# Chunked linear attention of the first half moved into the second input projection, with a first chunk's load one step ahead of its scores

## The chip, the core and the metric

The kernel runs on one NeuronCore of a Trainium2 chip: TensorE (PE, with its weight loads shown as PEld), VectorE (DVE), ScalarE (ACT), GpSimd (POOL), and SyncE (SP), whose queue issues the DMAs here. The metric is the device time of one execution in microseconds (us); lower is better. Times are compared as medians of several runs on one chip, and a profile shows one execution.

## The reference

One decoder block over 2048 positions of width 1024, all in float32. A normalised input goes through one input projection; its columns feed a gated linear attention (four heads, a forget gate of low rank) and a short gated convolution; both are joined by an output projection, and a gated feed-forward network follows.

```python
proj = h @ w_in[l]
p_q, p_k, p_v, p_g, p_a, c_b, c_c, c_h = jnp.split(proj, splits, axis=-1)
gate_logits = p_a @ w_gate_up[l] + b_gate[l]
log_a = jax.nn.log_sigmoid(gate_logits) / GATE_NORMALIZER
o = gla_chunked(q, k, v, log_a)
o = rmsnorm(o, gla_norm_g[l]) * jax.nn.silu(p_g)
u = c_c * c_h
o_conv = c_b * causal_depthwise_conv(u, conv_w[l])
x = x + jnp.concatenate([o_gla, o_conv], axis=-1) @ w_out[l]
h2 = rmsnorm(x, norm2_g[l])
x = x + (jax.nn.silu(h2 @ w_ffn_gate[l]) * (h2 @ w_ffn_up[l])) @ w_ffn_down[l]
return rmsnorm(x, norm_f_g)
```

Within a chunk the scores q k^T are masked and multiplied with v, and a state carried from chunk to chunk adds `q_t S_t`. The kernel uses chunks of 128 positions.

## The kernel before

The sequence is worked on in two halves of 1024 positions, each of two blocks of 512 (`b` = 0, 1 and 2, 3). Every product of a large matrix is a Strassen-like product of seven smaller ones (`PRODUCTS`: A11·B11, S1·T1, S2·T2, A12·B21, S3·T3, S4·B22, A22·T4), and each float32 factor is split into a high and a low part (`split`: ScalarE writes the high part, VectorE the rest), so that one product step is three matmuls (lines 447 to 449).

`unit` does the seven products for two column tiles of the weights: it loads 1 MB of raw weights (`raw`), mixes and splits them into seven quarters (`wq`), and multiplies each with one of the seven sorts of operand (`op`, four tiles each, 28 in all, in a pool `opp` of 28 slots). A product of the input projection is 12 matmuls, a unit 84. `in_proj(half)` runs over the units: k, q, two of v, two of g, then twice cc, ch, cb of the convolution. The first half has its first two units in a special opening, so `in_proj(0)` runs ten and `in_proj(1)` twelve. In the first half VectorE mixes the weights, in the second GpSimd.

The operands of the second half (`h1_ahead`) are made beside the first half's projection and kept in DRAM (`siB`, `siT`); `load_pairs(s_h1)` loads them back between the two projections. Since `opp` is full, each such load waits until the last unit of `in_proj(0)` has used the slot. The sorts T3, B22 and T4 are kept whole (256 KB) and split again after loading (`load_whole`); the others come as pairs (512 KB).

The attention of a half is a generator, `gla_half`. A chunk has three steps with a `yield` behind each: `gla_scores` (`sc` matmuls, masked copies into `scores` on VectorE, transposes `kt_ps` and `v_ps`, on ScalarE their evictions and the scaled state `carry`), `gla_outputs` (`o_ps`, `kv`, the new state, the norm), and `gla_finish` (transpose `ot`, gate, split, two stores to `sgla`). `gla_load` issues 14 DMAs of 64 KB for a chunk (`kq`, `ee`, `vt`, `gt`), and computes the exponentials of the decay and their products with k and q. `gate(half)` makes the decays of a half: 32 matmuls `a_ps`, four `z`, and for each `z` a chain of ScalarE and VectorE work with a scan (`forget_gate`), stored to `sd`.

What runs beside the projections stands in the list `background`, one generator after the other. Each product of a unit calls `tick`, which counts `pace` and, at every second product, does one step of the first generator in the list; `steady` adds a step at every fourth. A scheduler then sets the order of all instructions on each engine, by the program's order and its own model of time; engines keep that order. All DMAs here go through SyncE's one queue, in order.

Before the change, `gla_half(0)` is put into the list within `in_proj(0)`, after the g units, behind `h1_paced()`; its first three steps fall into the last unit of that projection. `gate(1)` comes next, at the start of `in_proj(1)`, and `gla_half(1)` follows after the g units of `in_proj(1)`; it ends within the output projection of the first half (`out_proj(0)`, four quarters of 96 matmuls). `out_proj(1)` reads what it stored.

Of the kernel before, what the change touches and what calls it, by code (L numbers as in the profile page):

```python
# [53 lines left out]
def tile_hymba_block(ctx, tc, x, xt, win, wa, wgu, wout, wffn, wdown, wdown_first, small, out):  # L54
# [83 lines left out]
    def bank(name="mm"):  # L138
        return ps.tile([P, PB], F32, name=name, tag="mm")
# [10 lines left out]
    def store(dst, src):  # L150
        return nc.sync.dma_start(dst, src)
# [5 lines left out]
    @contextmanager  # L157
    def behind(marks):

        with ExitStack() as stack:  # L160
            for m in marks:
                stack.enter_context(tc.issue_after(m.ins))
            yield
# [94 lines left out]


    background = []  # L260
    pace, ahead, hurry, steady = [0], [], [], []

    def step():
        while background:
            try:
                next(background[0])
                return
            except StopIteration:
                background.pop(0)

    def tick():
        pace[0] += 1
        if ordered:
            return
        if pace[0] % 2 == 0 or hurry:
            step()
            if steady and pace[0] % 4 == 0:
                step()
        elif ahead and pace[0] % 4 == 1:
            next(ahead[0], None)  # L280

# [9 lines left out]
    def unhurried():  # L291
        hurry.clear()
        steady.append(True)
        yield

    def h1_paced():
        with_marks.append(True)
        yield from h1_ahead()
        with_marks.clear()
        steady.clear()  # L300

    def drain_background(until=lambda: False):
        while background and not until():
            step()
# [210 lines left out]
    def settled(c, in_psum):  # L515

        if not in_psum:
            return c
        s = tt("c11")
        act.activation(s[:], c[:], AF.Copy)  # L520
        return s
# [3 lines left out]
    def silu(c, in_psum):  # L525
        s = tt("sg") if in_psum else c
        last_silu[:] = [act.activation(s[:], c[:], AF.Silu)]
        return s
# [404 lines left out]
    def gate(half, ops, mark=None):  # L933

        a = bank("a_ps")
        names = "B11", "T1", "B21", "B22"
        with behind([mark] if mark else []):
            for n in names:  # L940
                for k in range(4):
                    q = {"B11": 3 * k + 1, "T1": 3 * k, "B21": 2 * k + 13, "B22": 2 * k + 12}[n]
                    w = wa_sb[:, 32 * q : 32 * q + P]
                    for e in range(2):
                        pe.matmul(  # L945
                            a[:], w, ops[n][k][:, e, :],
                            start=(n, k, e) == ("B11", 0, 0),
                            stop=n == "B22" and k == 3 and e == 1, skip_group_check=True,
                        )
        if mark:  # L950
            yield

        stacks = []
        if half == 0:
            second_factor()
        for j in range(2):
            stack = bx[0].tile([96, PB], F32R, name="a_sb", tag="b")
            r, low = [slice(32 * n, 32 * n + 32) for n in (j, 1 - j)]
            with behind(held):
                act.activation(stack[r, :], a[r, :], AF.Copy)  # L960
                act.activation(stack[64:96, :], a[r, :], AF.Copy)
                dve.tensor_tensor(stack[low, :], a[r, :], stack[r, :].bitcast(F32), ALU.subtract)
            stacks.append(stack)
        yield
        for j in range(2):
            small = decays[2 * half + j] = [
                mtiny.tile([P, 2, PT], F32, name=n, tag=n, bufs=4) for n in ("em", "dn", "el")
            ]
            for i in range(2):
                z = bank("z")  # L970
                pe.matmul(
                    z[:], wgu_sb[:, i * P : (i + 1) * P], stacks[j][:], start=True, stop=True
                )
                forget_gate(2 * half + j, i, z, *small)
                yield
# [20 lines left out]
    def in_proj(half, ops, raw=None, between=(), rest=None):  # L996
        def units():
            if half == 0:
                yield unit(win[2], ops, raw=raw, between=between, rest=rest)
            for u in range(0 if half else 3, 12):  # L1000
                yield unit(win[u], ops, eng=pool if half else dve)

        units = units()
        for dst, i0 in ((s_kq, 0), (s_kq, 2), (s_v, 0), (s_v, 2)):
            if half == 0 and dst is s_kq:
                continue
            for r, j, c, p in next(units):
                store(dst[2 * half + j][i0 + r][:], settled(c, p)[:])
        for i0 in (0, 2):
            for r, j, c, p in next(units):  # L1010
                store(s_g[2 * half + j][i0 + r][:], silu(c, p)[:])
        background.append(gla_half(half))
        for i0 in (0, 2):
            cc = {(r, j): settled(c, p) for r, j, c, p in next(units)}
            ch = {(r, j): c for r, j, c, _ in next(units)}
            for r in range(2):
                i = i0 + r
                left = halo[:, i, :]
                for j in range(2):
                    s = tp.tile([P, PB + 2], F32, name="u", tag="t")  # L1020
                    dve.tensor_tensor(s[:, 2:], ch[r, j][:], cc[r, j][:], ALU.mult)
                    act.activation(s[:, 0:2], left, AF.Copy)
                    left = s[:, PB : PB + 2]
                    y = cc[r, j]
                    act.activation(y[:], s[:, 0:PB], AF.Copy, scale=col(C_CW + i))
                    for n in (1, 2):
                        dve.scalar_tensor_tensor(
                            y[:], s[:, n : n + PB], col(C_CW + 4 * n + i), y[:], ALU.mult, ALU.add
                        )
                if half == 0:  # L1030
                    act.activation(halo[:, i, :], left, AF.Copy)
            for r, j, c, _ in next(units):
                y = cc[r, j]
                dve.tensor_tensor(y[:], c[:], y[:], ALU.mult)
                hi = tp.tile([P, PB], F32R, name="hi", tag="t")
                split(y[:], hi[:], y[:].bitcast(F32R))
                dst = s_mix[2 * half + j][i0 + r]
                store(dst[:, 0, :], hi[:].bitcast(F32))
                store(dst[:, 1, :], y[:])


    def gla_half(half):
        chunks = [(b, t) for b in (2 * half, 2 * half + 1) for t in range(PT)]
        with tc.issue_after(last_silu[0].ins):
            tables = act.preload_act_table_set("natural_log_exp_and_others")
        with tc.issue_after(tables.ins):
            nxt = gla_load(*chunks[0])
        o = None
        for n, (b, t) in enumerate(chunks):
            cur = nxt  # L1050
            s = gla_scores(b, t, *cur)
            yield
            if o is not None:
                gla_finish(*chunks[n - 1], *o)
                yield
            if n + 1 < len(chunks):
                nxt = gla_load(*chunks[n + 1])
            o = gla_outputs(b, t, *s)
            yield
        gla_finish(b, t, *o)  # L1060
        done.add((b, t))
        yield
# [4 lines left out]
    def gla_load(b, t):  # L1067
        s = slice(t * P, (t + 1) * P)
        kq, e, vt, g = [bt(n, (P, 4, P)) for n in ("kq", "ee", "vt", "gt")]
        for dst, src in ((kq, s_kq[b]), (e[:, 2:4, :], s_d[b]), (vt, s_v[b]), (g, s_g[b])):  # L1070
            for i, r in enumerate(src):
                load(dst[:, i, :], r[:, s])
        act.activation(e[:, 0:2, :], e[:, 2:4, :], AF.Exp, scale=-1.0 / 16.0)
        act.activation(e[:, 2:4, :], e[:, 2:4, :], AF.Exp, scale=1.0 / 16.0)
        dve.tensor_tensor(kq[:, 0:2, :], kq[:, 0:2, :], e[:, 0:2, :], ALU.mult)
        dve.scalar_tensor_tensor(
            kq[:, 2:4, :], kq[:, 2:4, :], 0.125, e[:, 2:4, :], ALU.mult, ALU.mult
        )
        return kq, e, vt, g
# [412 lines left out]
    ops, raw, between, steps, rest = opening()  # L1492
# [4 lines left out]
        ]  # L1497
    )
    in_proj(0, ops, raw, between, rest)
    drain_background(lambda: len(background) < 2)  # L1500
    ops = load_pairs(s_h1)
    background.append(gate(1, ops))
    in_proj(1, ops)
    drain_background(lambda: (1, PT - 1) in done)
    ssq = out_proj(0, build_mix(0))
# [118 lines left out]
```

## Time and profile before

| what | us |
|---|---|
| median of 3 runs | 2073.3 |
| lowest and highest run | 2071.59, 2073.36 |
| the profiled execution | 2071.13 |
| its span (first to last instruction) | 2069.4 |
| TensorE busy in it | 2029.7 |
| VectorE, ScalarE, GpSimd busy | 1426.7, 971.2, 774.1 |

The mean granted TensorE clock of that execution is 0.994 of full speed. A row of a timeline reads: start and length in us, engine, source line, operation, tile written <- tiles read, shapes, count; in square brackets the idle time of the engine before it and what ended that. In a table of windows each row gives, for a stretch of time, busy us and number of instructions of PE, PEld, DVE, ACT and POOL, then the granted clock, the mean busy share of the 16 DMA engines and the GB/s they moved. "SPq" is SyncE's queue issuing a DMA. Line numbers are those of the kernel before.

### The profile page before, as it was taken

The numbers are of one execution on the slowest core, as the hardware profiler recorded it, in microseconds if no ns is written. First come the engines' busy times: TensorE is split into PE (matmuls) and PEld (weight loads), VectorE is DVE, ScalarE is ACT, GpSimd is POOL, SyncE is SP. The second block draws the span as 40 slices with busy tenths as digits, with TensorE's granted clock in tenths as the row PEclk, the third lists the DMA queues.
The fourth block names the chain that finished last, engine by engine and source line by source line (L and its number), as shares of the span: only waits on it lengthen the run. The fifth ranks groups of instructions, "written<-read, shape, count | busy, mean of one in ns | idle before, by whom it ended". The sixth has DMA issues, their size and how long they took to land.

```text
span 2069.4 us, 27151 instructions
## 1 busy us (share of the span) xinstructions
PE 2029.7 (98%) x9271; PEld 1666.8 (81%) x9271; DVE 1426.7 (69%) x2185; ACT 971.2 (47%) x1930; POOL 774.1 (37%) x566
## 2 busy tenths in 40 slices
PE   9999989999999999999999999999999999999997
PEld 8778768887888888888888888787888888878786
DVE  7878966568753686776676577776766666667774
ACT  6765555665542344444444452334434444453344
POOL 0000012222102474564564345533644554434544
PEclk9999999999999999999999999999999999999998
DMA  7356695434587783555454576477454444486653
GB/s 259 123 188 213 231 336 183 142 107 148 169 311 282 258 285 123 186 193 180 169 190 163 194 285 245 180 282 283 143 188 163 154 162 168 171 308 223 239 215 126
DMA packets 189739, 422.54 MB, mean 204 GB/s; under 512 B 19904, under 2 KB 65184, under 8 KB 180128
## 3 DMA queue, kind: packets, MB, share of 16 engines
q1 hardware_dynamic: 189600, 420.81, 57.3%
q8 instruction: 73, 1.20, 0.2%
q14 instruction: 66, 0.54, 0.1%
HBM read 276.02 MB, written 144.70 MB: 203 GB/s over the span
## 4 chain that ended last, share of the span: by engine, by line
PE 86%; DVE 6%; DMA 3%; ACT 2%; issue 1%; SPq 0%; POOL 0%; DVEq 0%; ACTq 0%
PE mm L447 24%; PE mm L449 24%; PE mm L448 24%; PE mm L1186 3%; PE mm L1189 3%; PE mm L1187 3%; DVE wq L194 1%; DMA op<-shT 1%; DMA op<-sa_B 1%; DVE op L194 1%; PE mm L731 1%; PE a_ps L945 1%; PE mm L733 1%; PE mm L732 1%; PE o_ps L1110 1%
## 5 line engine op out<-in xcount | busy, mean ns | idle before, releaser
L447 PE MATMUL mm<-op,wq 128*128 128x512 f32 x2467 | 963.6, 393 | 17.8 <-ACT wq L193 5.9
L448 PE MATMUL mm<-op,wq 128*128 128x512 f32 x2467 | 962.3, 390 | 2.4 <-DVE op L194 2.4
L449 PE MATMUL mm<-op,wq 128*128 128x512 f32 x2467 | 950.4, 390 | 0.9 <-DVE wq L194 0.8
L194 DVE TENSOR_TENSOR wq<-raw,wq 128x512 fp32r<-128x512 f32 (+2 forms) x612 | 489.3, 804 | 269.2 <-ACT wq L193 265.9
L193 ACT ACTIVATE wq<-raw 128x512 fp32r<-128x512 f32 (+2 forms) x612 | 355.9, 587 | 593.1 <-PE mm L449 453.9
L447 PEld LDWEIGHTS mm<-op,wq 128*128 128x128 f32 x2467 | 463.9, 188 | 123.1 <-ACT wq L193 8.6
L448 PEld LDWEIGHTS mm<-op,wq 128*128 128x128 f32 x2467 | 464.2, 188 | 101.4 <-DVE op L194 6.9
L449 PEld LDWEIGHTS mm<-op,wq 128*128 128x128 f32 x2467 | 464.1, 188 | 99.5 <-DVE wq L194 2.3
L422 POOL TENSOR_TENSOR s<-raw 128x512 f32<-128x512 f32 (+2 forms) x87 | 114.7, 1319 | 455.9 <-DVE wq L194 311.0
L422 POOL TENSOR_TENSOR raw<-raw 128x512 f32<-128x512 f32 (+2 forms) x174 | 228.7, 1320 | 122.8 <-DVE wq L194 117.5
L422 POOL TENSOR_TENSOR raw<-s,raw 128x512 f32<-128x512 f32 (+2 forms) x87 | 112.0, 1288 | 434.2 <-DVE wq L194 397.8
L476 DVE TENSOR_TENSOR c<-mm,c 128x512 f32<-128x512 f32 x196 | 134.4, 686 | 78.2 <-PE mm L449 76.6
L476 DVE TENSOR_TENSOR y<-mm,y 128x512 f32<-128x512 f32 x185 | 126.8, 687 | 83.9 <-PE mm L449 83.3
L1168 POOL TENSOR_TENSOR ssx<-ssx,q 128x512 f32<-128x512 f32 x52 | 76.9, 1493 | 155.4 <-ACT q L1167 155.1
L487 ACT ACTIVATE c<-mm 128x512 f32<-128x512 f32 x198 | 116.1, 588 | 17.2 <-PE mm L449 14.1
L1186 PE MATMUL mm<-op,wq 128*128 128x512 f32 x256 | 100.5, 394 | 0.0
L1187 PE MATMUL mm<-op,wq 128*128 128x512 f32 x256 | 99.7, 389 | 0.0
L193 ACT ACTIVATE wq<-s 128x512 fp32r<-128x512 f32 (+2 forms) x96 | 56.2, 585 | 86.1 <-PE mm L449 85.0
L194 DVE TENSOR_TENSOR wq<-s,wq 128x512 fp32r<-128x512 f32 (+2 forms) x96 | 81.3, 847 | 3.0 <-ACT wq L193 2.3
L194 DVE TENSOR_TENSOR op<-op 128x512 fp32r<-128x512 f32 x94 | 75.1, 828 | 8.3 <-ACT op L193 8.3
L1189 PE MATMUL mm<-op,wq 128*128 128x512 f32 x256 | 79.7, 390 | 0.0
L1381 POOL TENSOR_TENSOR y<-x,y 128x512 f32<-128x512 f32 x32 | 53.8, 1680 | 45.9 <-DVE y L476 41.7
(231 smaller groups left out, 1848.3 us busy)
## 6 DMA issues: line engine op xcount, KB each, us to landing
raw<-in_wffn_dram SPq DMA_DIRECT2D x44, 1024.0 KB, 5.9
sa_B<-so SPq DMA_DIRECT2D x47, 512.0 KB, 4.3
op<-sa_B SPq DMA_DIRECT2D x47, 512.0 KB, 7.0
raw<-in_win_dram SPq DMA_DIRECT2D x22, 1024.0 KB, 5.3
sa_T<-so SPq DMA_DIRECT2D x44, 512.0 KB, 4.4
op<-sa_T SPq DMA_DIRECT2D x44, 512.0 KB, 6.8
raw<-in_wdown_dram SPq DMA_DIRECT2D x24, 768.0 KB, 5.4
sx<-y SPq DMA_DIRECT2D x48, 256.0 KB, 3.8
```

The lines of the kernel that those rows point to most:

```text
L193: last_hi[:] = [act.activation(hi, src, AF.Copy)]
L194: last_lo[:] = [dve.tensor_tensor(lo, src, hi.bitcast(F32), ALU.subtract)]
L422: eng.tensor_tensor(*args)
L447: pe.matmul(o[:], wh, xh, start=first and k == 0, stop=False, skip_group_check=True)
L448: pe.matmul(o[:], wh, xl, start=False, stop=False, skip_group_check=True)
L449: return pe.matmul(o[:], wl, xh, start=False, stop=k == n - 1, skip_group_check=True)
L476: last_plus[:] = [dve.tensor_tensor(t[:], o[:], t[:], ALU.add)]
L487: last_out[:] = [act.activation(t[:], o[:], AF.Copy)]
L1168: pool.tensor_tensor(ssq[:], ssq[:], q[:], ALU.add)
L1186: pe.matmul(o[e, j][:], wh, m[:, 0, :], start=k == 0, stop=False)
L1187: pe.matmul(o[e, j][:], wh, m[:, 1, :], start=False, stop=False)
L1189: pe.matmul(o[e, j][:], wl, ops[k][j][:, 0, :], start=False, stop=k == KD - 1)
```

## The change

`gla_half(0)` is no longer put into the list within `in_proj(0)`. It is put there at the start of `in_proj(1)`, behind three empty steps (`pause(3)`) and ahead of `gate(1)`. While its first 14 steps run, a flag `hasty` adds a step at every fourth product, so three of four products carry one; after that it goes on at every second. And `gla_half`, of either half, gives up its turn once after the first chunk's load, so that the load and the scores of a first chunk are two steps.

```diff
-    pace, ahead, hurry, steady = [0], [], [], []
+    pace, ahead, hurry, steady, hasty = [0], [], [], [], []
@@ tick
             if steady and pace[0] % 4 == 0:
                 step()
+        elif hasty and pace[0] % 4 == 3:
+            step()
         elif ahead and pace[0] % 4 == 1:
             next(ahead[0], None)
@@
+    def pause(n):
+        for _ in range(n):
+            yield
+
+    def hastened(steps, n):
+        hasty.append(True)
+        for i, _ in enumerate(steps):
+            if i == n:
+                hasty.clear()
+            yield
@@ in_proj
-        background.append(gla_half(half))
+        if half:
+            background.append(gla_half(half))
@@ gla_half
             nxt = gla_load(*chunks[0])
+        yield
         o = None
@@
-    drain_background(lambda: len(background) < 2)
+    drain_background()
     ops = load_pairs(s_h1)
-    background.append(gate(1, ops))
+    background.extend([pause(3), hastened(gla_half(0), 14), gate(1, ops)])
     in_proj(1, ops)
```

The scheduler moves more than these lines say. Three places show it.

SyncE's queue, near the end of `in_proj(0)`, as a piece of the difference. `kq` and `ee` are loads of the first chunk, `siB` and `siT` the DRAM copies of the second half's operands.

```order
 L148 DMA kq<-sk_0_113 128x128
 L148 DMA kq<-sk_1_114 128x128
+L148 DMA op<-siB_0_441 128x1024
+L148 DMA op<-siB_1_442 128x1024
+L148 DMA op<-siB_2_443 128x1024
 L148 DMA kq<-sk_2_115 128x128
+L151 DMA siB_3_456<-lo 128x512
+L151 DMA siT_3_468<-t_2506 128x512
+L148 DMA op<-siB_3_444 128x1024
+L148 DMA op<-siT_0_445 128x1024
+L148 DMA op<-siT_1_446 128x1024
```

The operand loads, which stood behind all loads of the first two chunks, now stand behind two of the first chunk's.

SyncE's queue a little later, around the raw weights of the second unit of `in_proj(1)`. Before:

```order
L148 DMA gt<-sg_1_154 128x128
L148 DMA gt<-sg_2_155 128x128
L148 DMA gt<-sg_3_156 128x128
L148 DMA raw<-in_win_dram 128x2048
L148 DMA kq<-sk_0_113 128x128
```

and now, as a piece of the difference:

```order
+L148 DMA op<-siB_0_461 128x512
+L148 DMA op<-siB_1_462 128x512
+L148 DMA op<-siB_2_463 128x512
+L148 DMA raw<-in_win_dram 128x2048
+L148 DMA op<-siB_3_464 128x512
```

Before, these weights stood behind all operands and behind the fourteen loads of the third chunk; now they stand ahead of the last B22 operand (`siB_3_464`) and of the four T4 operands.

TensorE, at the product of the first unit of `in_proj(1)` that reads the T4 operands. The numbers tell the tiles apart: `wq_3059` and `wq_3062` are the last two quarters of that unit before the change, and `wq_2939` is the last one now; `wq_3053` is the second quarter of the unit after it. Before:

```order
L447 MATMUL mm_3080<-op_3017,wq_3059 128x512
L448 MATMUL mm_3080<-op_3017,wq_3059 128x512
L449 MATMUL mm_3080<-op_3017,wq_3059 128x512
L447 MATMUL mm_3065<-op_3021,wq_3062 128x512
L448 MATMUL mm_3065<-op_3021,wq_3062 128x512
L449 MATMUL mm_3065<-op_3021,wq_3062 128x512
```

and now (lines 460 to 462 are the same three as 447 to 449):

```order
L461 MATMUL mm_3110<-op_2848,wq_3053 128x512
L462 MATMUL mm_3110<-op_2848,wq_3053 128x512
L1107 MATMUL kt_ps_3131<-ident_87,kq_3086 128x128
L1110 MATMUL v_ps_3134<-ident_87,vt_3088 128x128 x4
L460 MATMUL mm_2942<-op_2898,wq_2939 128x512
L461 MATMUL mm_2942<-op_2898,wq_2939 128x512
```

The product with T4 followed the product with B22 directly; now the first two products of the next unit and the first chunk's scores and transposes stand between. From the first chunk's scores in the order before (in the last unit of `in_proj(0)`, behind that unit's first product), 143 matmuls of the projections lie before the last B22 operand is read in the new order, 156 before the first chunk's scores, and 168 before the first T4 operand. TensorE's order is the same in both up to those first scores, and from the feed-forward network on the order is the same again.

## The prediction

> **What bounds the kernel now.** I read the engine totals first, then what TensorE waited for between 240 and 480 us (the stretch in which the moved steps run), then that stretch cut into windows, then the instructions there.
>
> ```profile
> span 2069.4 us, 27151 instructions
> PE 2029.7 (98%) x9271; PEld 1666.8 (81%) x9271; DVE 1426.7 (69%) x2185; ACT 971.2 (47%) x1930; POOL 774.1 (37%) x566
> ```
>
> TensorE sets the time and is idle for only 2069.4 - 2029.7 = 39.7 us. A change that moves work and removes none can win only idle time, and time at a reduced clock. What TensorE waited for in the stretch (engine, line, releaser: us in total, times, longest):
>
> ```profile
> PE sc L1086 <- DVE kq L1076: 4.4, 2, 2.5
> PE mm L447 <- ACT wq L193: 4.0, 1, 4.0
> PE mm L448 <- DVE op L194: 1.8, 4, 0.8
> PE mm L447 <- ACT op L193: 1.2, 1, 1.2
> PE mm L447 <- DVE c L476: 0.6, 1, 0.6
> ```
>
> Two waits of the scores (one at the first chunk of each half), one for a weight split, several for the splitting of the next operands, and a short one for an eviction. The long ones lie here:
>
> ```profile
> 250.36 0.71 PE L1086 MATMUL sc<-kq 64*128 64x128 f32 x8 [1.89 <-DVE kq L1076]
> 295.48 0.50 PE L447 MATMUL mm<-op,wq 128*128 128x512 f32 x1 [1.21 <-ACT op L193]
> 307.01 0.50 PE L447 MATMUL mm<-op,wq 128*128 128x512 f32 x1 [4.04 <-ACT wq L193]
> 317.47 0.71 PE L1086 MATMUL sc<-kq 64*128 64x128 f32 x8
> 467.87 1.21 PE L1086 MATMUL sc<-kq 64*128 64x128 f32 x8 [2.47 <-DVE kq L1076]
> ```
>
> The windows (busy us and instructions of PE, PEld, DVE, ACT, POOL; then the granted TensorE clock, DMA share, GB/s):
>
> ```profile
> 240.00:248.00 8.00, 8.00 (x36) 6.42 (x35) 8.00 (x11) 3.74 (x9) 3.30 (x2) 1.00 0.67 233
> 248.00:260.00 12.00, 10.11 (x62) 8.04 (x61) 10.78 (x21) 7.73 (x21) 0.00 (x0) 1.00 0.52 141
> 260.00:296.00 36.00, 33.27 (x160) 25.29 (x158) 25.91 (x48) 20.75 (x48) 3.40 (x2) 1.00 1.03 392
> 296.00:304.00 8.00, 6.55 (x29) 4.38 (x29) 4.54 (x9) 4.31 (x8) 0.00 (x0) 0.79 0.65 182
> 304.00:312.00 8.00, 4.99 (x25) 4.51 (x26) 5.01 (x5) 3.14 (x10) 4.47 (x3) 0.79 0.92 272
> 451.00:466.00 15.00, 14.40 (x64) 11.54 (x62) 14.91 (x27) 11.43 (x27) 6.21 (x4) 1.00 0.46 157
> 466.00:472.00 6.00, 4.13 (x20) 3.49 (x21) 4.72 (x12) 3.68 (x9) 0.00 (x0) 0.72 0.47 134
> ```
>
> Three things are to be seen. From 260 to 296 us the DMA engines are full (share 1.03 at 392 GB/s), while before it they are half idle (0.52). After the stalls the clock is cut (0.79, 0.79, 0.72). And VectorE is full in 240 to 248 and 451 to 466 us (14.91 of 15). Why DMA starts late, and why the weights come late, stands in SyncE's queue:
>
> ```profile
> 257.17 1.86 SPq L148 DMA_DIRECT2D gt<-sg  x4
> 259.13 1.81 SPq L148 DMA_DIRECT2D op<-siB  x4
> 292.17 1.02 SPq L148 DMA_DIRECT2D op<-siT  x2
> 293.56 2.24 SPq L148 DMA_DIRECT2D kq<-sk  x4
> 299.36 1.85 SPq L148 DMA_DIRECT2D gt<-sg  x4
> 301.25 0.43 SPq L148 DMA_DIRECT2D raw<-in_win_dram  x1
> ```
>
> The next half's operands are first asked for at 259.13, behind the small loads of two chunks; the weights on which TensorE waits until 307.01 at 301.25, behind the fourteen loads of a third.
>
> **How much is lost there now.** In 240 to 248 us 36 large matmuls fill 8.00 us, 0.222 us each. From the end of work before the first scores (250.36 - 1.89 = 248.47) to the scores of the fourth chunk at 317.47 TensorE does this much of them:
>
> ```profile
> 248.47:317.47 69.00, 47.29 (x181) 0.95 0.89 308
> ```
>
> (of tile mm alone) 181 x 0.222 = 40.2 us. What the steps of a chunk take, by the pieces of the chain of waits around 500 to 520 us:
>
> ```profile
> 501.70 0.22 PE o_ps L1112 x2
> 501.93 0.59 PE kv L1117 x8
> 508.18 0.65 PE sc L1086 x8
> 508.82 0.37 PE kt_ps L1092 x2
> 509.19 0.44 PE v_ps L1095 x4
> 515.12 0.44 PE ot L1146 x4
> ```
>
> With eight of the o_ps pieces a chunk is 8 x 0.22 + 0.59 + 0.65 + 0.37 + 0.44 + 0.44 = 4.3 us; the first chunk has half the o_ps work, 3.4. Between those two points lie chunks 0, 1 and the third without its ot: 3.4 + 4.3 + 3.8 = 11.5 us. So 69.0 - 40.2 - 11.5 = 17.3 us are lost in one half-to-half boundary.
>
> **The change, part by part.** No matmul is added or dropped; the chunks' 11.5 us are done later, at the same price, so moving them is worth nothing by itself. (1) First scores of the first half: they move 156 matmuls on, their load is far ahead, and the 1.89 us wait goes. It is part of the 17.3.
>
> (2) The boundary. Operand loads now stand ahead of all but two of the first chunk's small loads. Each waits until the last unit of the first projection has used its slot; the first is free when that unit's first product ends, about 248.5, so loading starts some 11 us before the 259.13 of now. How soon is it through? The sizes:
>
> ```profile
> op<-siB SPq DMA_DIRECT2D x8, 512.0 KB, 8.3
> op<-siT SPq DMA_DIRECT2D x8, 512.0 KB, 10.0
> op<-siT SPq DMA_DIRECT2D x8, 256.0 KB, 5.9
> op<-siB SPq DMA_DIRECT2D x4, 256.0 KB, 5.1
> raw<-in_win_dram SPq DMA_DIRECT2D x22, 1024.0 KB, 5.3
> ```
>
> The 28 operands are 16 x 512 + 12 x 256 = 11264 KB. Up to the last B22 operand, itself counted, stand 24 of them (10240 KB), the next unit's weights (1024), eleven chunk loads of 64 KB and four 256 KB stores: 12992 KB or 13.3 MB, 34 us at 392 GB/s. From 247.5 that is 281.5, and with ScalarE's and VectorE's split (about 0.6 us each) near 283. TensorE, never waiting, would ask for it 143 matmuls after 248.47, at 280.2. So some 3 us are lost there. The last T4 operand comes 2.5 MB (6.5 us) later, near 289; the new order has put the next unit's first two products ahead of the product that reads T4, which is 168 matmuls on plus 1.5 us of the first chunk: 287.3, or 290 with the 3 us. Bounds: 0 lost, if TensorE itself is held up by 3 us elsewhere; 9, if the small loads among the big ones hold DMA to the mean of 260 to 304 us ((36 x 392 + 8 x 182) / 44 = 354 GB/s, 38 us), with a clock cut behind it. I take 4, nearest to the 3.0 us (1.8 + 1.2) of operand waits that the full DMA engines leave now.
>
> Behind operand loads that wait for TensorE, SyncE now holds the rest of the first chunk's loads, and ScalarE's exponential of that chunk waits for them with the third weight split of the coming unit behind it. About 4.9 MB stand ahead: 12.5 us, so 260; the split is used 105 matmuls on, at 272. It fits.
>
> (3) The weights of the next unit stand ahead of the last B22 operand and not behind T4 and fourteen chunk loads, so they land near 281, some 8 us before their use: the 4.04 us wait and the clock cut behind it (304 to 312 us) go. Both are in the 17.3; together (1) to (3) leave 4 of it: 13.3 us gained.
>
> On the clock: it was not cut in 248 to 260 us after one idle 1.89 us, and it was cut in 296 to 304 us after waits of which none was over 1.21. The Trainium skill (TensorE: Matmul & The Clock Gate, What's actually happening) has the cut come after an idle window of about 3.4 us; the row speaks against that, since broken waits were enough. By the page, waits broken like those expected here would carry no cut, and 4 us would be nearer to 3.
>
> (4) First scores of the second half: their load is now a step ahead, and the last matmul of the forget gates, whose work filled VectorE in 451 to 466 us, stands 84 matmuls (19 us) before them. The 2.47 us wait goes, and the cut (6.0 x (1 - 0.72) = 1.7): 4.2 us.
>
> (5) What it costs. The gates do not vanish: they move into the units whose convolution needs VectorE too. In 451 to 466 they needed all of it and TensorE still lost only 15.00 - 14.40 = 0.6; with the convolution beside them I take 1.5 (0 to 4). The built order has 17 activation-table loads for 15, the two new ones around the exponentials of a chunk between two silu evictions. A load in the trace:
>
> ```profile
> 396.95 0.62 ACT L193 ACTIVATE wq<-raw 128x512 fp32r<-128x512 f32 x1
> 397.59 1.28 ACT L527 ACT_TABLE_LOAD   x1
> 398.88 0.63 ACT L527 ACTIVATE c<-c 128x512 f32<-128x512 f32 x1
> ```
>
> 1.28 us each, 2.6 on ScalarE, in a place where seven such loads now leave TensorE the one wait of 0.6 on c; I take 1 (0 to 2.6). The Trainium skill (ScalarE: Activation LUTs, What ACT_TABLE_LOAD costs) adds a drain and gives about 2.66 us a switch, 5.3 for two; here the next activation starts at 398.88, 1.29 after the load, and the one before it ended at 397.57, so no drain is seen, and the sum goes by 1.28. Last, the hastened steps: o_ps follows its scores after 24 matmuls (5.3 us) where it mostly had 48. I take 1.5 (0 to 5; the rival below says more). The last chunk ends one quarter of the output projection later, with a quarter (96 matmuls, 21 us) left before the next projection; that one reads 1 MB in twelve matmuls (2.7 us), as fast as 392 GB/s brings it, so it needs only a lead, and has one: nothing.
>
> Sum: -13.3 - 4.2 + 1.5 + 1.0 + 1.5 = -13.5 us on an execution of 2071.1 (span 2069.4). That one lay 2.2 under the median of the three runs, 2073.3; so the median should come to 2073.3 - 13.5, about **2060 us**.
>
> **The rivals.** *Full recovery:* nothing is left at the boundary and the costs in (5) are covered: -17.3 - 4.2 + 1 = -20.5, 2053 us. For it: the next unit's products stand ready to fill. Against it: DMA must carry 13 MB in the 32 us that TensorE gives it, at the rate at which it is already full.
>
> *The stall only moves:* the chunks' 11.5 us of TensorE work used to cover loading; without it TensorE reaches the new operands sooner and waits at the full DMA engines for as long as it saved. Then (1) to (3) give nothing, (4) pays for (5), and the time is 2073. For it: share 1.03 already. Against it: the 11 us of earlier start and the half-idle DMA of 248 to 260 us.
>
> *Slower:* at three steps in four, the chain from scores over VectorE's two masked copies and ScalarE's evictions and carries to o_ps no longer fits between them, and TensorE, which keeps its order, waits in every hastened chunk. It decides when that chain takes over 5.7 us (24 matmuls and the ot between). Six chunks at 2.5 us (the longest wait of scores now) and a clock cut of 1.7 each are 25 us, less the 13.5: 2085. For it: scores and o_ps stood this close in few chunks before. Against it: the list of waits above has no row for o_ps, and VectorE is busy for 25.91 of 36 us and ScalarE for 20.75 there.
>
> **How the numbers follow.** A measurement of this kernel tells 0.2% (4 us) from no change. Chances: forecast 0.55 (its own range 2055 to 2066), full recovery 0.12, the stall moves 0.20, slower 0.13. Faster is the first two and a quarter of the third: 0.72; same 0.15; slower 0.13. The range reaches from full recovery into the moved stall and leaves out the slower case and a few in a hundred below: 2053 to 2073.
>
> **What would show it.** Right: no wait of sc on kq in either half; first operand load near 248; DMA full at once behind it; waits on op of 2 to 6 us near 275 to 290; no 4 us wait on wq; 250 to 315 us shorter by about 13 us when the moved chunks are counted. Wrong: operand waits over 10 us, rows of TensorE waiting for scores, carry or vt before o_ps, or VectorE full for 20 us where gates and convolution meet.

## The result and the profile after

| | median, us | lowest to highest | runs |
|---|---|---|---|
| before | 2072.45 | 2069.94 to 2073.36 | 4 |
| changed | 2061.74 | 2059.16 to 2063.03 | 4 |

The ratio is 0.9949, with a 95% interval of 0.9931 to 0.9966: 10.7 us faster, where 2060 was predicted and 13.5 us forecast. The profiled execution took 2061.84 us. Its first lines:

```profile
span 2060.1 us, 27151 instructions
PE 2023.8 (98%) x9271; PEld 1663.5 (81%) x9271; DVE 1429.7 (69%) x2185; ACT 971.3 (47%) x1932; POOL 770.3 (37%) x566
```

The same 9271 matmuls are in a span 9.3 us shorter. TensorE's idle time fell only from 39.7 to 36.3 us; its busy time fell by 5.9, since a matmul at half clock, or one that starts after a wait, counts as longer (0.50 us for the one at 277.42 us below, 0.39 for the next). What TensorE waited for between 230 and 520 us (engine, line, releaser: us in total, times, longest), and in a stretch of the feed-forward network, where the kernel before has no wait at all (770 to 800 us of its trace):

```profile
PE mm L460 <- DVE c L489: 3.4, 4, 1.6
PE mm L460 <- ACT c L500: 2.8, 2, 2.1
PE mm L461 <- DVE op L194: 0.2, 1, 0.2
```

```profile
PE mm L460 <- ACT c L500: 1.8, 1, 1.8
```

The waits of scores, the 4.0 us on weights and nearly all of those on operands are gone. What is left are waits for evictions, on lines 489 (VectorE) and 500 (ScalarE). Windows of the prediction again (busy us and instructions of PE, PEld, DVE, ACT, POOL; then clock, DMA share, GB/s):

```profile
248.00:260.00 12.00, 12.00 (x55) 9.95 (x54) 11.24 (x18) 6.41 (x13) 1.60 (x1) 1.00 0.98 371
260.00:296.00 36.00, 33.63 (x161) 26.30 (x160) 27.16 (x42) 20.51 (x41) 7.44 (x5) 1.00 0.93 328
296.00:304.00 8.00, 8.00 (x44) 6.39 (x43) 5.51 (x11) 5.48 (x19) 2.58 (x2) 1.00 0.95 315
304.00:312.00 8.00, 8.00 (x52) 6.65 (x50) 4.14 (x6) 3.17 (x10) 3.83 (x3) 1.00 0.53 163
466.00:472.00 6.00, 4.44 (x20) 3.33 (x19) 6.00 (x12) 3.25 (x9) 0.00 (x0) 1.00 0.44 137
```

From 248 to 260 us DMA is now almost full (0.98, before 0.52), and 296 to 312 us is full on TensorE at full clock. SyncE's queue shows why:

```profile
243.09 1.68 SPq L148 DMA_DIRECT2D op<-siB  x3
...
271.24 2.57 SPq L148 DMA_DIRECT2D op<-siB  x3
274.06 0.33 SPq L148 DMA_DIRECT2D raw<-in_win_dram  x1
274.79 0.32 SPq L148 DMA_DIRECT2D op<-siB  x1
...
283.45 0.39 SPq L148 DMA_DIRECT2D op<-siT  x1
```

The first operands are asked for at 243.09 (before: 259.13), the next unit's weights at 274.06 (before: 301.25).

**Where the time is lost, by stretch.** For the comparisons below I add up, from the trace, how far the starts of successive matmuls lie apart beyond the distance of an undisturbed one (0.227 us for 512 columns: 250 of them take 56.67 us; 0.110 for the narrow ones of a chunk). This takes in waits and half clock alike. The stretches are in us of each kernel's own span.

| lost, us | to 240 | 240-318 | 318-440 | 440-540 | 540-690 | 690-820 | rest | all |
|---|---|---|---|---|---|---|---|---|
| before | 11.3 | 15.8 | 1.9 | 4.2 | 0.3 | 1.0 | 19.6 | 54.2 |
| changed | 10.9 | 4.2 | 1.0 | 4.6 | 1.0 | 2.9 | 20.4 | 44.9 |

The difference, 9.3, is that of the spans. 11.6 us are won at the boundary of the two projections; about 1.9 are given back at 775 us, and every other stretch is within a microsecond.

### The profile page after: what moved, and what is told of

It reads as the page before. It is cut to its first block, busy times and chain, and to the rows that moved or that the text cites. A ratio compares the mean times of both kernels' runs of the same rounds, so it can differ in the third digit from the quotient of the medians.

```text
span 2060.1 us, 27151 instructions
## 1 busy us (share of the span) xinstructions
PE 2023.8 (98%) x9271; PEld 1663.5 (81%) x9271; DVE 1429.7 (69%) x2185; ACT 971.3 (47%) x1932; POOL 770.3 (37%) x566
## 4 chain that ended last, share of the span: by engine, by line
PE 82%; DVE 8%; DMA 5%; ACT 2%; issue 2%; POOL 1%; SPq 0%; DVEq 0%; ACTq 0%; POOLq 0%
PE mm L460 24%; PE mm L462 23%; PE mm L461 23%; PE mm L1201 2%; PE mm L1202 2%; PE mm L1204 2%; DVE wq L194 1%; DVE op L194 1%; DMA raw<-in_win_dram 1%; DMA op<-shT 1%; DMA op<-siT 1%; DVE h L882 1%; PE a_ps L958 1%; PE mm L744 1%; PE mm L746 1%
```

## The experiments

Three groups: one part of the change alone, the change without one part, and other orders. The ratio is that to the kernel before on the same chip, with its 95% interval; the losses are of one profiled execution each, by the measure above.

| kernel | median | ratio | 240-318 | 318-440 | 440-540 | 540-690 | 690-820 |
|---|---|---|---|---|---|---|---|
| yield_only | 2070.48 | 0.9996 (0.9987 to 1.0004) | 17.8 | 2.0 | 1.5 | 0.0 | 1.1 |
| pool_queue | 2072.88 | 1.0007 (0.9996 to 1.0018) | 19.1 | 1.1 | 2.6 | 0.5 | 1.0 |
| move_plain | 2076.39 | 1.0029 (1.0019 to 1.0039) | 13.4 | 0.7 | 11.6 | 0.1 | 5.1 |
| no_yield | 2063.35 | 0.9962 (0.9950 to 0.9975) | 3.1 | 0.2 | 11.2 | 0.9 | 0.8 |
| no_pause | 2064.49 | 0.9965 (0.9953 to 0.9977) | 12.0 | 1.7 | 1.3 | 0.9 | 0.2 |
| no_haste | 2073.59 | 1.0007 (0.9998 to 1.0015) | 2.2 | 1.2 | 3.4 | 17.1 | 0.5 |
| late_weights | 2068.94 | 0.9988 (0.9978 to 0.9999) | 11.3 | 0.9 | 4.7 | 1.0 | 3.1 |
| after_again | 2060.30 | 0.9958 (0.9945 to 0.9972) | 3.4 | 1.2 | 4.6 | 0.9 | 3.1 |
| gate_first | 2060.86 | 0.9952 (0.9937 to 0.9968) | 1.4 | 5.9 | 0.5 | 0.9 | 4.0 |
| haste_all | 2060.96 | 0.9947 (0.9935 to 0.9959) | 3.5 | 1.9 | 5.7 | 0.9 | 0.4 |
| gate_pause | 2067.00 | 0.9982 (0.9973 to 0.9990) | 1.4 | 5.3 | 5.7 | 7.6 | 1.0 |
| interleaved | 2056.03 | 0.9930 (0.9918 to 0.9942) | 1.2 | 4.3 | -0.1 | 1.0 | 0.2 |

### One part alone

**yield_only**: the extra step, and nothing else.

```diff
             nxt = gla_load(*chunks[0])
+        yield
         o = None
```

> The kernel before with nothing but the extra step between a first chunk's load and its scores. Theory (queue order): SyncE still issues all chunk loads of two chunks ahead of the second half's operands and the next weights behind the third chunk's, so the loss between 285 and 312 us (some 12 us by gaps between matmuls) stays; only the two waits of first scores go, 1.9 us and 2.5 us with its clock cut of 1.7: 2072.4 - 6 = 2066, ratio 0.997. Rival (the first scores' waits are the gain): the whole of it shows here, 2062, ratio 0.995. Third (the waits only move to the next matmul): 2072.

Measured: 0.9996, the third theory's number, though not by its way. The waits of scores are gone, and the second half's stretch fell from 4.2 to 1.5 us, but the boundary lost 2.0 more. TensorE's waits from 240 to 318 us:

```profile
PE mm L447 <- ACT wq L193: 4.3, 1, 4.3
PE mm L448 <- DVE op L194: 2.3, 4, 1.2
PE mm L447 <- DMA op<-siB: 1.5, 1, 1.5
PE mm L447 <- DMA op<-siT: 1.3, 4, 0.4
PE mm L447 <- ACT op L193: 1.2, 1, 1.2
```

Operands (2.3, 1.5, 1.3, 1.2) and weights (4.3) are waited for longer: TensorE no longer loses 1.9 us at the first scores, the first operands are asked for no earlier (259.62 us), and so it stands longer at them. Here a wait ahead of a longer wait on a transfer was worth nothing by itself.

**pool_queue**: the attention stays where it was; the loads of its first three chunks leave SyncE's queue for GpSimd's.

```diff
-                load(dst[:, i, :], r[:, s])
+                (pool.dma_start if b == 0 and t < 3 else load)(dst[:, i, :], r[:, s])
```

> The kernel before, with the loads of the first three chunks (42 DMAs of 64 KB) issued from GpSimd's queue and no longer from SyncE's. TensorE's order is nearly that of before (first scores at matmul 972 for 960). Theory (queue order): operand loads start near 245 us, the weights of the next unit come ahead of T4, and of the 15 us lost between 248 and 312 some 10 go; the second half's wait of 2.5 us with its cut stays: 2062 to 2064, ratio 0.995. Rival (the moved work is the gain, or DMA bandwidth is): no gain, 2071 to 2074. Against both: GpSimd's instructions stand behind DMA issues that wait for buffers, and may be late.

Measured: no gain; my theory in this form fell. The operands did come early (first issue at 241.96 us) and none was waited for, and 0.8 us is left of the 4.0 on weights, but the stretch lost 19.1 us. Its waits, and a window:

```profile
PE sc L1086 <- issue: 5.8, 1, 5.8
PE sc L1086 <- DVE kq L1076: 2.8, 1, 2.8
...
```

```profile
248.00:260.00 12.00, 9.14 (x33) 7.10 (x34) 6.63 (x13) 3.44 (x9) 7.29 (x14) 0.72 1.03 387
```

Now the scores of the first two chunks wait. The 2.8 us are the price of the queue: DMA is full from 248 us on (1.03, 387 GB/s), and the first chunk's last `ee` load took 7.0 us, where it took 2.0 before, and landed at 252.43 us, 6.4 later than before. The 5.8 us are not, or not directly. The second chunk's last `ee` load landed at 263.05 us, and TensorE came to that chunk's scores at 276.37. What was late is ScalarE's exponential, behind a split that waited for VectorE:

```profile
276.14 0.63 ACT L193 ACTIVATE hi<-c 128x512 fp32r<-128x512 f32 x1 [3.85 <-DVE c L1034]
276.68 0.40 ACT L1073 ACTIVATE ee<-ee 128x256 f32<-128x256 f32 x1
```

The product for `kq` that TensorE waits for then ended on VectorE at about 282 us. So early operands alone gained nothing in this order, and putting one sort of load ahead made another late; but the longer wait came through the queues of ScalarE and VectorE, 13 us after the loads had landed, so this run does not show that the chunks have to go for want of DMA alone.

**move_plain**: the attention moved, without empty steps, haste or extra step.

```diff
-        background.append(gla_half(half))
+        if half:
+            background.append(gla_half(half))
...
-    drain_background(lambda: len(background) < 2)
+    drain_background()
-    background.append(gate(1, ops))
+    background.extend([gla_half(0), gate(1, ops)])
```

> The kernel before with the attention of the first half put at the start of the second input projection and nothing else: no empty steps, no haste, no extra step. Operand loads lead SyncE's queue as in the changed kernel, but the weights of the second unit stand behind the T4 operands and some 25 chunk loads, and the product with T4 is not deferred. Theory (operands, next weights and a late first chunk are needed together): a wait on weights of 3 to 5 us near 285 to 295 us and waits on operands, with a clock cut: 2066 to 2068, ratio 0.997 to 0.998. Rival (moving the attention is enough): 2062, ratio 0.995.

Measured: slower than before. Waits from 240 to 318 and from 440 to 540 us:

```profile
PE mm L460 <- ACT wq L193: 4.8, 1, 4.8
PE mm L460 <- ACT op L193: 1.8, 1, 1.8
```

```profile
PE mm L460 <- DVE c L489: 2.8, 1, 2.8
PE mm L462 <- DVE wq L194: 2.5, 1, 2.5
...
```

The wait on weights came as expected (4.8), and the boundary still gains 2.4 us on the kernel before. What I had not counted is the second stretch: the gates come later still (their first matmul after 1632 of the projections' matmuls in the built order, 1608 in the changed kernel, 1524 before), among the convolution units, and 11.6 us are lost in that stretch. Lateness alone does not set the price: in no_haste below they begin after 1728 and the stretch loses 3.4. Another 4.1 us more than before are lost between 690 and 820 us.

### The change without one part

**no_yield** (the `yield` above removed from the changed kernel) and **no_pause** (`pause(3)` removed).

> The changed kernel without the extra step. SyncE's queue at the boundary is that of the changed kernel. Theory (queue order): 240 to 315 us keep the gain; the second half's first scores stand 120 matmuls behind the forget gates' last (108 before the change, 144 with it), so a wait of 0 to 2.5 us and perhaps a clock cut of 1.7 come back there: 2062 to 2066. Rival (the first scores' waits are the gain): 6 us are given back, 2068 or more.

> The changed kernel without the three empty steps. First scores come after 1059 matmuls (1116 with the steps), the next unit's weights again stand behind T4 and its product with T4 is not deferred. Theory: the same wait on weights of 3 to 5 us and operand waits as in the kernel with the bare move: 2066. Rival (the empty steps are without effect): 2062, ratio 0.995.

Without the extra step the boundary keeps its gain (3.1 lost) and the median is in the expected band, but the loss in the second half was 11.2, not 0 to 4.2 above the changed kernel's 4.6. Its waits from 440 to 540 us:

```profile
PE mm L460 <- DVE c L489: 5.3, 1, 5.3
PE sc L1100 <- DVE kq L1090: 2.5, 1, 2.5
```

The 2.5 us of scores are back, as they were before; the 5.3 us is an eviction behind the gates' scans in VectorE's queue, as at 468 us in the changed kernel, only longer. This stretch lost 6.6 us more than in the changed kernel, yet the profiled spans are 2060.6 and 2060.1 us: no_yield lost less in every other stretch of the table, 2.1 of it between 690 and 820 us, where the changed kernel has a new stall, and 1.4 before 240 us, where it had no cut of the clock. So the ratios hardly differ (0.9962 against 0.9949 and 0.9958, with intervals that overlap), and the times do not show that the extra step is worth anything on the whole.

Without the empty steps the weights are late again: 4.3 us on `wq` and 1.6 on `op`, with 10.2 us of half clock, and 12.0 us lost at the boundary against 4.2. The ratio is 0.9965, between the two theories' numbers. The stretch from 440 to 540 us loses only 1.3 there: the whole sequence runs earlier, and the gates begin after 1524 matmuls, as before the change. Its interval overlaps that of the changed kernel's repeat on the same chip, so the empty steps pay at the boundary (7.8 us), and what they are worth on the whole is not shown.

**no_haste**: the attention at every second product throughout.

```diff
-    background.extend([pause(3), hastened(gla_half(0), 14), gate(1, ops)])
+    background.extend([pause(3), gla_half(0), gate(1, ops)])
```

> The changed kernel with its attention steps at every second product throughout. The boundary's queue is that of the changed kernel. Theory: the boundary's gain stays, and the evictions that TensorE waits for at 312, 388 and 500 us (0.6, 0.9, 0.9) shrink a little; but the last transpose of the second half falls on the last matmul of the first half's output projection, so the chain behind it (gate, split, two stores, a load of it) stands open before the next projection: 6 to 10 us lost there, 2066 to 2070. Rival (haste only costs): no stall there, 2059.

Measured: the whole gain is lost, in one wait from 640 to 690 us:

```profile
PE mm L1201 <- DMA op<-sgla: 13.3, 1, 13.3
```

The mechanism is the expected one, at 13.3 us for the 6 to 10 that I gave it. Haste is what pays for the later start.

**late_weights**: the changed kernel, with the weights of one unit issued after the last T4 operand.

```diff
-        raw_loads.append(load(raw, src))
+        with behind(late_marks[-1:]):
+            raw_loads.append(load(raw, src))
+        late_marks.clear()
...
-        load(o[:, 1, :].bitcast(F32), src[:])
+        whole_loads.append(load(o[:, 1, :].bitcast(F32), src[:]))
...
+                if half and u == 1:
+                    late_marks.append(whole_loads[-1])
```

> The changed kernel with one load held back: the second unit's weights are issued behind the last T4 operand. Theory: the weights' place is a term of its own; they are asked for near 288 and land near 293 us, where TensorE reaches them near 283 to 286: waits on T4 of 1 to 2 us and on weights of 4 to 5 us and a clock cut, so 6 to 8 us more between 270 and 310 us: 2066 to 2068, ratio 0.997 to 0.998. Rival (the early operand loads alone make the gain): 2062 to 2063.

Measured: the load was issued at 285.15 us instead of 274.06, and the boundary lost 11.3 us instead of 4.2: 7.1 for one load's place (against the changed kernel's repeat, 7.9). The waits from 240 to 318 us (lines lie 3 further down, 1 in `split`):

```profile
PE mm L463 <- ACT op L194: 2.7, 2, 1.8
PE mm L463 <- ACT c L503: 1.7, 1, 1.7
PE mm L463 <- ACT wq L194: 1.6, 1, 1.6
```

Only 1.6 is named as a wait on weights; 2.7 is on operands, because without these weights the order has no next unit's products to put ahead of the product that reads T4. The clock cut that I expected did not come, and the median lies 8.6 us above the repeat's, a little over the expected band. The place of the weights is worth most of the boundary's gain, by what it lets TensorE do while T4 is on its way.

**after_again**: the changed kernel itself.

> The changed kernel itself, timed on the chip of the three kernels with it. Ratio 0.995; the waits of 2.1 us at 277 us and 1.6 us at 468 us come again, since both follow from a fixed order; the 1.8 us at 775 us behind an activation-table load, which the kernel before shows without a wait in the same order, comes in some executions only.

Measured: 0.9958. The stalls at 277 and 468 us came again, and so did the one of 1.8 us in the feed-forward network. That last expectation of mine was wrong: it comes in every profiled execution of the changed kernel, late_weights, gate_first and move_plain, and of the other nine kernels, the one before included, none waits more than 0.4 us there. In the changed kernel ScalarE runs:

```profile
759.19 0.63 ACT L193 ACTIVATE op<-h 128x512 fp32r<-128x512 f32 x1 [4.86 <-DMA h<-sfB]
...
772.32 1.28 ACT L540 ACT_TABLE_LOAD   x1
773.61 0.63 ACT L540 ACTIVATE c<-c 128x512 f32<-128x512 f32 x1
774.15 0.58 ACT L500 ACTIVATE c<-mm 128x512 f32<-128x512 f32 x1
```

TensorE waits 1.77 us, until 774.78, for the last of these. Before, the same instructions came 2.6 us earlier against TensorE (their table load 63.5 us after the 3400th matmul, 66.1 now) and hid. The delay goes back to the load `h<-sfB` of the first row. In the four kernels with the stall it is issued 44.9 to 45.4 us after the 3400th matmul, and ScalarE stands 3.8 to 5.3 us for it; in the other nine it is issued after 41.0 to 42.3 us, and ScalarE stands 0.6 to 2.3 us. The scheduler has moved splits of operands about on ScalarE just ahead of this, 300 us behind the change, and the loads stand differently in SyncE's queue; which of these makes the load late was not tried apart.

### Other orders

**gate_first**, **haste_all**, **gate_pause** and **interleaved** differ from the changed kernel in one line:

```diff
-    background.extend([pause(3), hastened(gla_half(0), 14), gate(1, ops)])
+    background.extend([pause(3), gate(1, ops), hastened(gla_half(0), 14)])              # gate_first
+    background.extend([pause(3), hastened(gla_half(0), 99), gate(1, ops)])              # haste_all
+    background.extend([pause(3), gate(1, ops), pause(3), hastened(gla_half(0), 99)])    # gate_pause
+    background.extend([pause(3), hastened(in_turn(gla_half(0), gate(1, ops)), 24)])     # interleaved
```

> The changed kernel with the second half's forget gates ahead of the hastened attention, not behind it. No chunk load stands between the operand loads, and the gates meet the k units, not the convolution. Theory: the wait of 2.1 us at 277 us for an eviction behind late operand splits shrinks, the waits of 1.6 and 0.8 us on VectorE at 468 and 489 us go: 2058 to 2060, ratio 0.993. Rival (the gates only move their cost): VectorE is late with evictions or splits between 265 and 300 us, 2 to 4 us: 2062 to 2064.

> The changed kernel with both halves' attention at three steps in four, to the end. Theory: the chain from scores to o_ps fits into 24 matmuls, no wait of o_ps appears, and each of the eleven or so further hastened chunks costs under 0.3 us: 2061 to 2065. Rival (the slower case of the prediction: the chain does not fit beside the rest): waits of o_ps or ot of 1 to 2.5 us in most of these chunks: 2075 to 2085.

> Gates first, then three empty steps, then the attention of both halves at three steps in four. Theory: the VectorE waits of 1.8 us at 333 and 0.8 us at 409 us (gates, then the convolution beside chunks) shrink with the distance, haste costs nothing: 2056 to 2060, ratio 0.993. Rival (the chunks only meet the convolution later): 2062.

> The changed kernel with the gates' five steps and the attention's first steps taken in turn, hastened, so that gates neither meet the convolution nor come all at once. Theory: no chunk load between the operands, no wait of VectorE at 468 and 489 us, and the waits of 1.8 and 1.4 us that gates ahead of the attention showed at 320 to 333 us are halved: 2056 to 2058, ratio 0.993. Rival (VectorE's work is the same wherever it stands): 2060 to 2062.

gate_first: both theories were right in part. 240 to 318 us lost 1.4 and 440 to 540 us 0.5, as the first said; 318 to 440 us lost 5.9 for 1.0, later than the second said. The sum is no gain that can be told.

haste_all: no wait of `o_ps` or `ot`. The chain from scores to `o_ps` fits into some 24 matmuls in all of these chunks; the slower case of the prediction does not hold here. Two things it did not foresee: 3.9 us behind the gates' scans on VectorE at 447 us (busy for 8.00 us from 440 to 448), and no stall in the feed-forward network (0.4 lost for 2.9).

gate_pause: missed, at 2067.0 us for 2056 to 2060. From 440 to 690 us TensorE waits for `osb`, which `ot` reads:

```profile
PE ot L1161 <- DVE osb L1154: 8.2, 3, 4.3
```

Two of the three (1.4 us at 469 us, 2.5 at 497) stand beside the convolution. They may be the slower case's mechanism one step further down the chain, though haste_all, with hastened chunks beside the convolution too, has none of them. The longest, at 613 us beside the output projection, is a late load once more:

```profile
607.45 1.15 ACT L193 ACTIVATE wq<-raw 128x512 fp32r<-128x512 f32 x2 [7.19 <-DMA raw<-in_wout_dram]
608.50 0.26 ACT L1149 ACTIVATE sq<-o_ps 128x128 f32<-128x128 f32 x1
```

ScalarE stood 7.19 us for weights of the output projection, with the squares from which the chunk's norm and then `osb` are made queued behind their split.

interleaved: 2056.0 us, as its theory had it, faster than the kernel before and, on the same chip, faster than the changed kernel: 0.9930 (0.9918 to 0.9942) against 0.9958 (0.9945 to 0.9972). Its waits from 240 to 540 us:

```profile
PE mm L460 <- ACT c L500: 2.2, 1, 2.2
PE mm L460 <- ACT wq L193: 0.7, 1, 0.7
```

Beside the repeat of the changed kernel it saves 2.2 us at the boundary, 4.7 between 440 and 540 us and 2.9 in the feed-forward network (which is the scheduler's doing, not that of the idea), and loses 3.1 more between 318 and 440 and 2.9 more behind 820 us; the profiled span is 3.8 us shorter. The 2.2 us left stands behind ScalarE, which sat 3.94 us waiting for a load of `ee` with an eviction queued behind it.

## Why the prediction was right

The sum forecast -13.5 us. By the measure above:

| term | forecast | measured |
|---|---|---|
| (1) to (3), the boundary | 17.3 lost, 4 left: -13.3 | 15.8 lost, 4.2 left: -11.6 |
| (4), first scores of the second half | -4.2 | gone: -4.1 |
| (5), gates beside the convolution | +1.5 (0 to 4) | 1.9 at 468 us + 1.1 at 489 us: +2.9 |
| (5), two more table loads | +1.0 | nothing to be seen |
| (5), hastened steps | +1.5 | nothing to be seen |
| not foreseen: 499 us, and behind 513 us | 0 | 1.0 + 0.5 = +1.5 |
| not foreseen: 690 to 820 us | 0 | +1.9 |
| elsewhere | 0 | +0.1 |

The trace gained 9.3 us for the 13.5 forecast, the medians 10.7. That the total came as near as this is in part luck: 2.5 us of costs that did not come stand against 3.4 that were not foreseen. The 17.3 itself was too large. Its 0.222 us a matmul divides 8.00 us by 36, of which the window cuts off parts; at 0.227 the 181 matmuls take 0.8 us more, which is half of the difference to 15.8.

**The boundary.** The mechanism held: operands and weights come earlier, and late operands are what is left. The size of the 4 us left was right and its place was not. I had TensorE wait for the last B22 operand near 283 us and for T4 near 290. The loads began at 243.09, ahead of the 247.5 of my sum (the first slots came free earlier than I had reckoned; my text has 248.5), but from 243 to 279 us DMA moved 357 GB/s and not 392. The two errors cancelled: the last B22 operand landed at 281.98 us and the last T4 operand at 290.62, for 281.5 and near 289. TensorE did not wait for B22 because it had by then lost 2.1 us at 277 us, the case of the forecast's lower bound; for T4 there is one wait of 0.2. Those 2.1 us are late operands too, through ScalarE:

```profile
273.45 1.25 ACT L193 ACTIVATE op<-op 128x512 fp32r<-128x512 f32 x2 [1.90 <-DMA op<-siT]
274.74 0.60 ACT L500 ACTIVATE c<-mm 128x512 f32<-128x512 f32 x1
275.23 0.62 ACT L193 ACTIVATE wq<-raw 128x512 fp32r<-128x512 f32 x1
275.75 1.14 ACT L193 ACTIVATE op<-op 128x512 fp32r<-128x512 f32 x2
276.79 0.58 ACT L500 ACTIVATE c<-mm 128x512 f32<-128x512 f32 x1
```

```profile
277.42 0.50 PE L460 MATMUL mm<-op,wq 128*128 128x512 f32 x1 [2.11 <-ACT c L500]
```

ScalarE stands idle for 1.90 us until a `siT` operand lands, with an eviction behind it in its queue; then it splits two operands, evicts, splits a weight tile and two more operands, and only then evicts the bank for which TensorE waits. The page names `c` on ScalarE, not DMA; the row before it tells whose delay it is. That gate_first, with no chunk load between the operands, has 0.7 us there agrees with it.

**The weights** were a term of their own, as (3) had it, and larger than I made it: I gave their lateness the 4.04 us and a clock cut, and late_weights showed 7.1.

**What the change needs.** I had put the gain down to the order of SyncE's queue. That is half of it. In pool_queue early operands without moved chunks gave nothing (2.8 us of its waits are chunk loads made late, 5.8 came through the queues of ScalarE and VectorE); move_plain and no_pause show that moved chunks with late weights leave 12 to 13 us, no_haste that a later start without haste gives all of it back at the end, and no_yield that the extra step keeps the second half's scores from waiting. The bare move is slower than the kernel before.

**The gates.** The gates' cost was within its range and above its value: from 466 to 472 us VectorE was busy for 6.00 of 6 us. In its queue

```profile
463.88 2.42 DVE L1000 TENSOR_TENSOR_SCAN g<-ones,g 128x128 f32<-128x128 f32 x4
466.23 0.66 DVE L1035 TENSOR_TENSOR u<-c,c 128x512 f32<-128x512 f32 x1
466.81 0.74 DVE L1041 SCALAR_TENSOR_TENSOR c<-u,sml,c 128x512 f32<-128x512 f32 x1
467.47 0.68 DVE L489 TENSOR_TENSOR c<-mm,c 128x512 f32<-128x512 f32 x1
```

four scans of a gate and two steps of the convolution stand ahead of the eviction of line 489 that releases TensorE at 468.20, after 1.56 us; the second wait is 0.78 at 489 us. gate_first, which has the gates elsewhere and the second half's chunks at the same place in TensorE's order, has neither.

**Table loads and haste.** The table loads are 17 for 15, as said, and the one wait among them is 0.6 on `c`, as before: the cover held. The hastened steps brought no wait of `o_ps`: they end near 387 us, and 318 to 440 us lost 1.0 us, for 1.9 before. The gap of 1.0 us at 499 us is an eviction behind ScalarE's `carry` and splits, in the second half's attention, which is not hastened. gate_first does not have it, so it goes with where the gates stand; the 0.5 us behind 513 us gate_first has too.

**The rivals.** Full recovery asked for no loss at the boundary; interleaved comes near to it (1.2). The stall that only moves is what yield_only shows, and pool_queue in part: it was the right fear for half a change. The slower case did not hold for the order of the change.

## What to carry to other kernels

When a stretch is short of DMA, an early load can make another late: what counts is which loads the stretch contains at all, and one 1 MB load's place among them was worth 7 us. Read the row ahead of a wait on an eviction: an engine that keeps its order and waits for a transfer passes the delay on under another name, as ScalarE did at 277 us, in the feed-forward network and in gate_pause. After moving work in a kernel that a scheduler orders, look through the whole trace for new waits, far from the move too: here 2 us came 300 us later from instructions that nobody had touched.

## What was unexpected of the hardware

A wait of the same length cuts TensorE's clock in one execution and not in another. All fourteen profiled executions have a wait of 1.9 us at about 81 us and one of 1.8 to 1.9 at about 123 us of their span. The windows behind them, first of gate_first, then of the changed kernel (the clock is the third number from the end):

```profile
84.00:88.00 4.00, 3.92 (x11) 3.09 (x11) 3.77 (x8) 3.94 (x10) 0.00 (x0) 0.58 0.69 182
...
126.00:130.00 4.00, 3.54 (x17) 2.83 (x18) 3.79 (x12) 3.88 (x6) 0.00 (x0) 1.00 0.07 27
```

```profile
84.00:88.00 4.00, 4.00 (x18) 3.29 (x19) 3.72 (x7) 3.93 (x9) 0.00 (x0) 1.00 0.77 223
...
126.00:130.00 4.00, 4.00 (x14) 3.25 (x13) 3.40 (x9) 2.13 (x4) 0.00 (x0) 0.57 0.34 131
```

In 4 of the 14 the clock was halved after the first, in 3 after the second, in 7 after neither, each time for 3.41 us. From 240 to 318 us, late_weights has four waits of 0.9 to 1.8 us within 17 us and no cut; no_pause has 10.2 us of half clock, three times 3.41, for one wait of 1.6 and one of 4.3. The Trainium skill (TensorE: Matmul & The Clock Gate, What's actually happening) has a free-running window of 3413 ns, and the cut after an idle one of about that length. The length of the cuts agrees, and a free-running window would explain the chance in it; that the window must be idle throughout does not agree with cuts after 1.9 us of waiting. No run here shows the window itself. So in these runs the clock's share of a term is a matter of odds: a cut of 3.41 us at half clock costs 1.7 us, and a single execution can have one more or one fewer.
